# Down-weight sums moved to the tail's second half, and a late scan operand taken from SBUF

## The chip, the cores and the metric

The kernel runs on one core of a Trainium2 chip. The metric is the device time of one execution in microseconds. The engines are named as in the profile: PE (TensorE matmul) and PEld (its weight load), DVE (VectorE), ACT (ScalarE), POOL (GpSimd) and SP, whose queue issues most DMAs.

## The reference

One decoder layer over 2048 tokens of width 1024, all in float32. What the change touches is the stick-breaking attention and the feed-forward part.

```python
z = einsum("bhqd,bhkd->bhqk", qb, kh) * scale          # scale = 1/8, key before query only
log_1m_beta = where(mask, log_sigmoid(-z), 0.0)
between = cumsum(log_1m_beta, reverse) - log_1m_beta
attn = where(mask, exp(log_sigmoid(z) + between), 0.0)  # sigmoid(z) * running product of (1 - sigmoid)
out = einsum("bhqk,bhkd->bhqd", attn, vh)

gt = einsum("bsd,df->bsf", f_in, w_gate)                # d = 1024, f = 2816
up = einsum("bsd,df->bsf", f_in, w_up)
f = einsum("bsf,fd->bsd", silu(gt) * up, w_down)
h = h + rmsnorm(f)
```

Around it stand a norm and an input projection, a gated convolution of width 31 over half of the mixing channels, and an output projection of convolution and attention side by side.

## The kernel before, in words

Matrix products in full precision are made of three: each operand is split into a rounded part H and a remainder L (ACT makes H, DVE or POOL makes L), and PE adds L·H, H·H and H·L in one PSUM bank.

**The trunk.** Tokens come in four groups of 512. The list `PLAN` (line 39) walks through main steps: `prep` and `in` (input projection) for each group, `mixc`/`outc` and `mixa`/`outa` (the convolution's and the attention's half of the output projection), and pieces of the feed-forward (`fprep`, `c11`, `p4`). Each has a cost, and the running sum of costs is a position. Three side generators are drawn along: the attention, the convolution's taps, and `sums`. For each a line of points (`ATTN`, `TAPS`, `SUMS`, lines 69 to 71) says which share of it is to be done at which position; `beside` steps a side until it has reached its share. This sets the order in which instructions are written. A scheduler then reorders them by its own timeline, except where `keep_in_program_order` holds them.

**The attention** (`attn`, line 534) goes group by group, head by head, and for each head through the key chunks from the diagonal to the first; a head and a chunk make a unit of four steps. A step of `scores` multiplies into a bank `z` (two banks), lets ACT take sigmoid(-z) into `om` and sigmoid(z) into `A`, lets DVE run a scan over `om` backwards (line 572), and POOL multiplies `A` by the scanned `om`. The scan is a multiply with the second step bypassed, so its second tensor is read and not used: it is a broadcast of z's first column, from PSUM. Its first element is the previous chunk's product, put there by small POOL copies (`pv`, lines 567 and 575). A step of `values` then transposes `A` on PE (`at`), splits it into TH and TL, and multiplies with V into `o`. After a head come `pf` (fold of halves), and after each pair of heads a norm (`ot`) and a transpose back (`po`, `ma`). The attention of the last group feeds the last half of the output projection, in the tail's first lines.

**The feed-forward** uses a Strassen-like scheme of seven products per 2x2 block. So sums and differences of weight blocks are needed beforehand: `sums` (line 838) makes them on POOL, from pieces of 128x512 that SP loads, and stores them to DRAM: for `w_gate` and `w_up` under the key "S", for `w_down` under "wd". Three buffers `sum` are in use. There are 15 units of work for each of 11 blocks (`HF`), 10 for the first two matrices and 5 for the down matrix, spread along `SUMS`.

**The tail.** When the attention is done, its PSUM pools close. `five` (line 1096) makes five products for each of 44 blocks (token groups 0 and 2, each standing for two groups of 512; 11 column blocks; gate and up). Blocks 0 to 21 are the first half, 22 to 43 the second. A block's weights come by SP into `raw`, ACT makes wH, POOL makes wL (line 1067), and PE and DVE are held in program order. `behind` and `todo` place other work behind a block's second product. Results for the down product are kept in a list `late` and stored by `flush`, two per product. The buffers `x2` (two each of xH and xL) hold operands of products 6 and 5 in the first half and are free in the second.

**The last stage** (from line 1229) makes the seven down products: `fetch` (line 1244) loads a weight piece and a piece of u, and makes their H and L in buffers taken from `x2`; PE accumulates in `dps`.

Of the kernel before, what the change touches and what calls it, by code (L numbers as in the profile page):

```python
# [9 lines left out]
F32 = mybir.dt.float32  # L10
# [55 lines left out]
    ("outc", 3, 22),  # L66
)

ATTN = ((46, 0.0), (890, 1.0))
TAPS = ((30, 0.0), (130, 0.168), (170, 0.25), (260, 0.418), (300, 0.5), (410, 0.668), (450, 0.75), (650, 0.918), (700, 1.0))  # L70
SUMS = ((330, 0.0), (900, 1.0))

# [66 lines left out]
def layer_kernel(ctx: ExitStack, tc: tile.TileContext, x, xT, g_pre_mix, w_in, conv_w, conv_b, ln_g, ln_b,  # L139
# [394 lines left out]
    def attn(g):  # L534
# [20 lines left out]
        def scores(u, j):  # L555
            hd_ = heads[u["h"]]
            diag = u["c"] == g
            w = (j + 1) * P if diag else G
            K = u["K"]
            z = pp.tile([P, G], F32, tag="z", name="z")  # L560
            js = slice(j * P, (j + 1) * P)
            nc.tensor.matmul(z[:, 0:w], hd_["QL"][:, js], K[:, 0:w], start=True, stop=False)  # L562
            nc.tensor.matmul(z[:, 0:w], hd_["QH"][:, js], K[:, 0:w], start=False, stop=True)  # L563
            if diag:
                nc.vector.tensor_tensor(z[:, w - P:w], z[:, w - P:w], msk, ALU.add)  # L565
            om = ap.tile([P, G + 1], F32, tag="om", name="om", bufs=NOM)
            nc.gpsimd.tensor_copy(om[:, G:G + 1], hd_["prev"][j])
            nc.scalar.activation(om[:, G - w:G], z[:, 0:w], AF.Sigmoid, scale=-0.125)  # L568
            a = ap.tile([P, G], F32, tag="A", name="A", bufs=NA)
            nc.scalar.activation(a[:, 0:w], z[:, 0:w], AF.Sigmoid, scale=0.125)  # L570
            r = om[:, G - w:G + 1][:, ::-1]
            nc.vector.tensor_tensor_scan(r, r, z[:, 0:1].to_broadcast([P, w + 1]), one, ALU.mult, ALU.bypass)  # L572
            nc.gpsimd.tensor_tensor(a[:, 0:w], a[:, 0:w], om[:, G - w + 1:G + 1], ALU.mult)  # L573
            pv = sp.tile([P, 1], F32, tag="pv", name="pv", bufs=8)
            nc.gpsimd.tensor_copy(pv, om[:, G - w:G - w + 1])
            hd_["prev"][j] = pv
            u["A"].append(a)
            return w
# [175 lines left out]
    def four(t):  # L754
        return [t[:, i, :] for i in range(4)]
# [80 lines left out]
    def sums():  # L836

        def piece(w, j, e):
            t = fup.tile([P, G], F32, tag="sum", name="sum", bufs=3)
            nc.sync.dma_start(t, w[j][:, e * G:(e + 1) * G])  # L840
            return t

        late = []

        def combine(c, a, b, op, *key):
            nc.gpsimd.tensor_tensor(c, a, b, op)  # L846
            late.append((c, *key))

        def flush(n):
            while len(late) > n:  # L850
                t, kind, *key, m = late.pop(0)
                if kind == "S":
                    ns = (6, 7) if m in (6, 7) else (5, 3)
                    part(t, ns.index(m), 2, kind, *key, ns)
                else:
                    store(t, kind, *key, m)

        for j in range(HF):
            for i, w in enumerate(W):
                a21, a22, a11 = piece(w, j + HF, 0), piece(w, j + HF, 1), piece(w, j, 0)  # L860
                yield 1
                combine(a22, a21, a22, add, "S", i, j, 5)
                yield 1
                combine(a21, a21, a11, sub, "S", i, j, 7)
                combine(a11, a22, a11, sub, "S", i, j, 6)
                yield 1
                flush(0)
                a12 = piece(w, j, 1)
                yield 1
                combine(a12, a12, a11, sub, "S", i, j, 3)  # L870
                yield 1
                flush(0)
        for j in range(HF):
            b12, b11, b22 = piece(w_down, j, 1), piece(w_down, j, 0), piece(w_down, j + HF, 1)
            yield 1
            combine(b11, b12, b11, sub, "wd", j, 5)
            yield 1
            combine(b12, b12, b22, sub, "wd", j, 7)
            combine(b22, b22, b11, sub, "wd", j, 6)
            yield 1  # L880
            flush(0)
            b21 = piece(w_down, j + HF, 0)
            yield 1
            combine(b21, b21, b22, sub, "wd", j, 4)
            yield 1
            flush(0)

    def input_sums(g, k, tmp, banks=bank, t4=None):

# [56 lines left out]

    attn_s = Side(chain(attn(g) for g in range(NG)), 1 / (2 * NH * P * sum(16 * g + 10 for g in range(NG))), ("attn",))
    taps_s = Side(chain(taps(g) for g in range(NG)), 1 / (NG * (CB * CW + 3 * (TAPLAG + LAG * TT))), ("taps", "conv"))
    sums_s = Side(sums(), 1 / (15 * HF))
    fns = {"prep": (prep, 8), "qkv": (lambda g: inproj(g, qkv), 12), "gv": (lambda g: inproj(g, gv), 8),  # L950
           "in": (lambda g: inproj(g, both), 20),
           "mixc": (lambda g: mixed(g, 0), 1), "outc": (lambda g: outproj(g, 0), 4),
# [45 lines left out]
    with ExitStack() as E:  # L998
# [113 lines left out]
        def five(early, todo):  # L1112
# [85 lines left out]
                fn(*args)  # L1198
            next(more_h.pop())
            assert next(more, None) is None  # L1200
            for _ in range(9):
                flush(2)

        operands(0, [(6, x2), (5, x2), (7, e[4:6]), (3, e[0:2])])
        R = []
        last = NG - 2

        def steps():

# [18 lines left out]
        todo = {n: [(next, more)] * (1 if n < 5 else 2 - n % 2) for n in range(17)}  # L1228
        todo[17] = todo[18] = [(next, more)]
        todo[2 * HF - 1] = [(operands, last, [(3, e[0:2])], nc.gpsimd)]  # L1230
        five({2 * HF - 1: [(operands, last, [(7, e[4:6])])]}, todo)


# [164 lines left out]
```

## Time and profile before

| | |
|---|---|
| runs | 2579.35 us median of 3 (2574.46 to 2581.54) |
| the profiled execution's own time | 2579.23 us |
| its span, first to last instruction | 2577.5 us |
| mean granted TensorE clock | 0.977 |
| DVE, ACT, POOL busy | 70%, 50%, 58% |
| DMA in all | 657.32 MB, 255 GB/s |

A matmul of 512 columns has a duration of about 0.40 us in the rows, but they are pipelined and start about 0.23 us apart. Rows of a group give the line, the engine and the operation, the output and inputs by the program's names, the shapes and the count; then the busy time in us, the mean of one in ns, and the idle time of the engine just before, with what ended it. A row of waits names the waiting engine and line, and behind the arrow who ended the wait.

### The profile page before, as it was taken

The page shows a single profiled execution, that of the slowest core. Times are in us where ns is not written, and L with a number is a line of the kernel's source. Part 1 is how long each engine was busy: PE and PEld are TensorE (multiplying, and loading weights), DVE is VectorE, ACT ScalarE, POOL GpSimd, SP SyncE. Part 2 cuts the span into 40 slices and gives each one's busy share as a digit, 9 for nine tenths or more (in the row PEclk, how much of TensorE's full clock was granted, in tenths as well). Part 3 has the DMA queues.
Part 4 walks back from the last instruction along what each step waited for, and adds up shares of the span by engine and source line. Part 5 has one row for each costly group of instructions (what it writes and reads, how often), then busy time and mean ns, then how long its engine had stood idle before and what let it go on. Part 6 is the DMA issues. An engine that isn't in the chain of part 4 may idle for free.

```text
span 2577.5 us, 35682 instructions
## 1 busy us (share of the span) xinstructions
PE 2430.0 (94%) x11156; PEld 1963.3 (76%) x11156; DVE 1793.3 (70%) x2321; ACT 1291.5 (50%) x2398; POOL 1482.5 (58%) x1844
## 2 busy tenths in 40 slices
PE   7999989998999998999999979999999999998997
PEld 6878767776777776887788857777788878887886
DVE  5797689967997798887544547766655655557556
ACT  4455555655555655667666645332332233454543
POOL 5764668556755776639533228755443444567556
PEclk9999989998999899999999989999999999999999
DMA  9989877988898998857777746977656667668655
GB/s 360 303 301 311 287 244 260 369 262 272 273 328 287 314 329 285 275 189 230 263 257 243 242 140 235 340 265 234 213 189 201 199 200 266 195 189 286 204 188 171
DMA packets 289182, 657.32 MB, mean 255 GB/s; under 512 B 33888, under 2 KB 42080, under 8 KB 288992
## 3 DMA queue, kind: packets, MB, share of 16 engines
q1 hardware_dynamic: 264704, 622.01, 72.0%
q10 hardware_dynamic: 24288, 33.04, 3.5%
q8 instruction: 88, 1.44, 0.2%
q14 instruction: 102, 0.84, 0.1%
HBM read 460.92 MB, written 193.99 MB: 254 GB/s over the span
## 4 chain that ended last, share of the span: by engine, by line
PE 52%; DVE 11%; POOL 5%; DMA 4%; issue 3%; ACT 2%; SPq 0%; POOLq 0%; ACTq 0%; DVEq 0%
PE b L762 17%; PE dps L762 13%; PE c L762 8%; DVE cv L476 3%; DVE om L572 2%; PE at L589 2%; PE p L762 1%; PE ops L688 1%; PE ops L689 1%; PE ops L690 1%; PE o L595 1%; PE z L562 1%; PE o L594 1%; PE z L563 1%; DVE TL L249 1%
## 5 line engine op out<-in xcount | busy, mean ns | idle before, releaser
L573 POOL TENSOR_TENSOR A<-A,om 128x512 f32<-128x512 f32 (+2 forms) x320 | 313.7, 980 | 415.9 <-DVE om L572 364.3
L572 DVE TENSOR_TENSOR_SCAN om<-om,one,z 128x513 f32<-128x513 f32 (+2 forms) x320 | 351.3, 1112 | 114.5 <-ACT A L570 103.2
L1067 POOL TENSOR_TENSOR wL<-raw,wH 128x512 fp32r<-128x512 f32 x176 | 255.6, 1478 | 262.9 <-issue 164.6
L476 DVE SCALAR_TENSOR_TENSOR cv<-glu,cw,cv 128x512 f32<-128x512 f32 x464 | 346.6, 747 | 6.7
L1257 DVE TENSOR_TENSOR xL__22001<-t__22003,xH__22000 128x512 fp32r<-128x512 f32 x154 | 199.3, 1302 | 159.5 <-ACT xH__22000 L1256 159.3
L1255 POOL TENSOR_TENSOR xL__21999<-t__22002,xH__21998 128x512 fp32r<-128x512 f32 x154 | 207.8, 1354 | 173.3 <-ACT xH__21998 L1254 172.7
L256 PE MATMUL inps<-xH,wL 128*128 128x512 f32 x640 | 260.8, 408 | 12.9 <-ACT sg L422 11.0
L249 DVE TENSOR_TENSOR TL<-at,TH 128x512 fp32r<-128x512 f32 (+1 forms) x320 | 188.2, 598 | 110.3 <-ACT TH L248 109.8
L260 PE MATMUL inps<-xL,wH 128*128 128x512 f32 x640 | 258.4, 405 | 0.5 <-DVE xL L392 0.5
L258 PE MATMUL inps<-xH,wH 128*128 128x512 f32 x640 | 258.6, 405 | 0.0
L762 PE MATMUL dps<-xH__21998,xL__22001 128*128 128x512 f32 x616 | 240.9, 391 | 8.1 <-DVE xL__22001 L1257 7.2
L568 ACT ACTIVATE om<-z 128x512 f32<-128x512 f32 (+2 forms) x320 | 171.6, 539 | 153.0 <-DVE z L565 70.8
L762 PE MATMUL dps<-xL__21999,xH__22000 128*128 128x512 f32 x616 | 240.6, 391 | 2.2 <-POOL xL__21999 L1255 2.2
L762 PE MATMUL dps<-xH__21998,xH__22000 128*128 128x512 f32 x616 | 240.2, 390 | 0.0
L846 POOL TENSOR_TENSOR sum<-sum 128x512 f32<-128x512 f32 x132 | 171.8, 1302 | 89.3 <-DMA sum<-in_w_up_dram 33.4
L248 ACT ACTIVATE TH<-at 128x512 fp32r<-128x512 f32 (+1 forms) x320 | 168.2, 547 | 106.3 <-PE at L589 102.4
L1254 ACT ACTIVATE xH__21998<-t__22002 128x512 fp32r<-128x512 f32 x154 | 97.1, 631 | 231.9 <-POOL xL__21999 L1255 151.5
L589 PE MATMUL at<-idr,A 128*128 128x128 f32 x1088 | 192.1, 280 | 10.5 <-POOL A L573 9.3
L210 ACT ACTIVATE wH<-raw 128x1024 fp32r<-128x1024 f32 x156 | 165.8, 1065 | 53.5 <-DMA raw<-in_w_in_dram 19.1
L570 ACT ACTIVATE A<-z 128x512 f32<-128x512 f32 (+2 forms) x320 | 168.4, 542 | 21.0 <-PE at L589 13.6
L589 PEld LDWEIGHTS at<-idr,A 128*128 128x128 f32 x1088 | 142.0, 144 | 48.5 <-POOL A L573 12.4
L1066 ACT ACTIVATE wH<-raw 128x512 fp32r<-128x512 f32 x176 | 101.1, 623 | 154.8 <-PE b L762 77.1
(296 smaller groups left out, 6226.3 us busy)
## 6 DMA issues: line engine op xcount, KB each, us to landing
wL<-wL SPq DMA_DIRECT2D x156, 512.0 KB, 5.2
raw<-in_w_in_dram SPq DMA_DIRECT2D x80, 512.0 KB, 6.0
t__22003<-u SPq DMA_DIRECT2D x154, 256.0 KB, 2.8
c<-c ACTq DMA_DIRECT2D x88, 256.0 KB, 4.6
t__22002<-wd SPq DMA_DIRECT2D x88, 256.0 KB, 2.9
K<-kd SPq DMA_DIRECT2D x80, 256.0 KB, 4.6
V<-vd SPq DMA_DIRECT2D x80, 256.0 KB, 4.5
u<-accf SPq DMA_DIRECT2D x22, 768.0 KB, 4.2
```

The costliest lines, as they stand in the source:

```text
L249: nc.vector.tensor_tensor(L, ps, H.bitcast(F32), ALU.subtract)
L256: nc.tensor.matmul(ps, WL[:, kc], aH[t](k), start=k == 0, stop=False)
L258: nc.tensor.matmul(ps, WH[:, kc], aH[t](k), start=False, stop=False)
L260: nc.tensor.matmul(ps, WH[:, kc], aL[t](k), start=False, stop=k == KT - 1)
L476: nc.vector.scalar_tensor_tensor(to, gl[c][:, k:k + G], cw[:, c, k:k + 1], a, ALU.mult, ALU.add))
L572: nc.vector.tensor_tensor_scan(r, r, z[:, 0:1].to_broadcast([P, w + 1]), one, ALU.mult, ALU.bypass)
L573: nc.gpsimd.tensor_tensor(a[:, 0:w], a[:, 0:w], om[:, G - w + 1:G + 1], ALU.mult)
L589: nc.tensor.transpose(pt[:, j * P:(j + 1) * P], u["A"][j][:, b * P:(b + 1) * P], id32)
L762: return nc.tensor.matmul(ps, a, b, skip_group_check=True, **flags)
L1067: nc.gpsimd.tensor_tensor(l, t, f32(h), sub)
L1255: nc.gpsimd.tensor_tensor(WL, w, f32(WH), sub)
L1257: nc.vector.tensor_tensor(UL, t, f32(UH), sub)
```

## The change

Four edits:

1. `ATTN` ends at position 870 instead of 890.
2. The down matrix's part leaves `sums`, whose scale becomes 1/(10·HF); `SUMS` is unchanged.
3. A new generator `down_sums` makes the same sums inside the tail, two steps in each of blocks 22 to 43 and one behind the last: per column block four loads, four POOL operations, four stores through `late`. Its 16 buffers are the slices of `x2`. Its POOL operations are held in program order. Twelve rounds of `flush` instead of nine close the stage.
4. In the last group, for heads 4 to 7, the scan's unused second tensor is a broadcast of `one`, a column of ones in SBUF, instead of z's first column.

```diff
-ATTN = ((46, 0.0), (890, 1.0))
+ATTN = ((46, 0.0), (870, 1.0))
...
+            late = g == NG - 1 and u["h"] >= NH // 2
...
-            nc.vector.tensor_tensor_scan(r, r, z[:, 0:1].to_broadcast([P, w + 1]), one, ALU.mult, ALU.bypass)
+            nc.vector.tensor_tensor_scan(r, r, (one if late else z[:, 0:1]).to_broadcast([P, w + 1]), one, ALU.mult, ALU.bypass)
...
-        for j in range(HF):
-            b12, b11, b22 = piece(w_down, j, 1), piece(w_down, j, 0), piece(w_down, j + HF, 1)
-            yield 1
-            combine(b11, b12, b11, sub, "wd", j, 5)
-            yield 1
-            combine(b12, b12, b22, sub, "wd", j, 7)
-            combine(b22, b22, b11, sub, "wd", j, 6)
-            yield 1
-            flush(0)
-            b21 = piece(w_down, j + HF, 0)
-            yield 1
-            combine(b21, b21, b22, sub, "wd", j, 4)
-            yield 1
-            flush(0)
...
-    sums_s = Side(sums(), 1 / (15 * HF))
+    sums_s = Side(sums(), 1 / (10 * HF))
...
-            for _ in range(9):
+            next(more_wd)
+            for _ in range(12):
                 flush(2)
...
+        def down_sums():
+
+            wd = cycle([p for _ in range(2) for t in operand(*x2, dt=F32) for p in four(t)])
+
+            def piece(j, e, c):
+                t = next(wd)
+                nc.sync.dma_start(t, w_down[j][:, c * G:(c + 1) * G])
+                return t
+
+            def pinned(*args):
+                tc.keep_in_program_order(nc.gpsimd.tensor_tensor(*args))
+
+            def get(j):
+                return piece(j, 0, 1), piece(j, 0, 0), piece(j + HF, 0, 1), piece(j + HF, 0, 0)
+
+            nxt = get(0)
+            yield
+            for j in range(HF):
+                b12, b11, b22, b21 = nxt
+                pinned(b11, b12, b11, sub)
+                late.append([1, b11, "wd", j, 5])
+                yield
+                pinned(b12, b12, b22, sub)
+                late.append([1, b12, "wd", j, 7])
+                yield
+                pinned(b22, b22, b11, sub)
+                late.append([1, b22, "wd", j, 6])
+                yield
+                pinned(b21, b21, b22, sub)
+                late.append([1, b21, "wd", j, 4])
+                yield
+                if j + 1 < HF:
+                    nxt = get(j + 1)
...
+        more_wd = down_sums()
+        for n in range(2 * HF, 4 * HF):
+            todo[n] = todo.get(n, []) + [(next, more_wd)] * 2
```

The scheduler orders the whole trunk anew, so nearly every queue differs. Three places carry the prediction's steps; behind each row stand the engines and DMA queues that it waits for.

PE, end of the attention, before: `ops` is the first half of the last output projection, `z` the last unit's scores, `o`, `at` its values. The last `ops` row and what follows:

```order
L690 MATMUL ops_17368<-wL_17245,xH_17206 128x512
L562 MATMUL z_16877<-K_16873,QL_16280 128x512 [waits DMAHW4_49,DVE_49]
L563 MATMUL z_16877<-K_16873,QH_16279 128x512
L594 MATMUL o_16487<-TH_16844,V_16472 128x512 [waits Activation_49]
L562 MATMUL z_16945<-K_16873,QL_16280 128x512 [waits DVE_49]
L563 MATMUL z_16945<-K_16873,QH_16279 128x512
L595 MATMUL o_16487<-TL_16845,V_16472 128x512 [waits DVE_49]
```

PE, the same unit's first scores in the change, in the midst of `ops`:

```order
L691 MATMUL ops_17120<-wL_17027,xH_16988 128x512
L563 MATMUL z_16631<-K_16627,QL_15958 128x512 [waits DMAHW2_49,Activation_49]
L564 MATMUL z_16631<-K_16627,QH_15957 128x512
L563 MATMUL z_16691<-K_16627,QL_15958 128x512 [waits Activation_49]
L564 MATMUL z_16691<-K_16627,QH_15957 128x512
L595 MATMUL o_16209<-TH_16606,V_16194 128x512 [waits Activation_49]
L590 MATMUL at_16643<-idr_72,A_16527 128x128 [waits Pool_49]
L689 MATMUL ops_17134<-wH_17020,xL_16989 128x512 [waits Activation_49]
```

Before, all four z's of the last unit stand behind the last `ops` row and wait for DVE; 60 rows come between that row and the last half of the projection. In the change they wait for ACT and stand ahead of the last `ops` row, behind which 43 rows are left.

POOL in the tail's second half, before, one burst of wL for a block and the start of the next:

```order
L1067 TENSOR_TENSOR wL_21701<-raw2_21633,wH_21700 128x512 [waits DMAHW2_49,Activation_49,Pool_49]
L1067 TENSOR_TENSOR wL_21701<-raw2_21633,wH_21700 128x512 [waits Activation_49]
L1067 TENSOR_TENSOR wL_21763<-raw_21740,wH_21762 128x512 [waits DMAHW5_49,Activation_49,Pool_49]
L1067 TENSOR_TENSOR wL_21763<-raw_21740,wH_21762 128x512 [waits Activation_49]
L1067 TENSOR_TENSOR wL_21797<-raw2_21742,wH_21796 128x512 [waits DMAHW2_49,Activation_49]
```

and in the change:

```order
L1054 TENSOR_TENSOR wL_21732<-raw2_21667,wH_21731 128x512 [waits DMAHW3_49,Activation_49]
L1054 TENSOR_TENSOR wL_21732<-raw2_21667,wH_21731 128x512 [waits Activation_49]
L1206 TENSOR_TENSOR xL__19709<-xL__19709 128x512 [waits Pool_49] x2
L1054 TENSOR_TENSOR wL_21799<-raw_21768,wH_21798 128x512 [waits DMAHW4_49,Activation_49]
L1054 TENSOR_TENSOR wL_21799<-raw_21768,wH_21798 128x512 [waits Activation_49]
```

Two sums now stand between two bursts.

ACT at the start of the last stage, in the change: L1279 makes the H of the weights, L1281 (line 1256 before) the H of u.

```order
L1279 ACTIVATE xH__21958<-t0__21962 128x512 [waits DMAHW7_49]
L1279 ACTIVATE xH__21958<-t0__21962 128x512 [waits DMAHW2_49]
L1281 ACTIVATE xH__21960<-t1__21963 128x512 [waits DMAHW5_49,DMAHW3_49,DMAHW6_49,DMAHW1_49,Pool_49]
L1281 ACTIVATE xH__21960<-t1__21963 128x512
L1281 ACTIVATE xH__21960<-t1__21963 128x512 [waits DMAHW0_49]
```

The first H of u waits for POOL and for the stores of the last column block's four sums, which lie in its buffer; before, it waited for its own load alone.

## The prediction

> **What bounds the kernel now.** I read the page's first lines, then TensorE's busy time by stage, then who ended TensorE's idle time in the stages that the change touches, and last the built order of before and of the change.
>
> ```profile
> span 2577.5 us, 35682 instructions
> PE 2430.0 (94%) x11156; PEld 1963.3 (76%) x11156; DVE 1793.3 (70%) x2321; ACT 1291.5 (50%) x2398; POOL 1482.5 (58%) x1844
> ```
>
> TensorE (PE) is the bound: 147.5 us of the span are not covered by it, and that is all that an edit which adds and removes no matmul can win, beside time at a lower granted clock. The stages (columns: PE, weight loads, DVE, ACT, POOL busy, then granted clock, DMA share, GB/s):
>
> ```profile
> 658.00:1044.00 386.00, 355.82 (x1735) 286.16 (x1734) 341.86 (x470) 220.45 (x411) 262.94 (x381) 0.98 0.88 303
> 1044.00:1248.00 204.00, 200.59 (x988) 163.73 (x987) 154.66 (x201) 139.50 (x264) 132.21 (x209) 1.00 0.67 221
> 1248.00:1485.00 237.00, 231.87 (x1144) 189.51 (x1143) 118.53 (x154) 155.23 (x284) 82.64 (x184) 1.00 0.76 258
> 1485.00:1531.00 46.00, 32.01 (x126) 24.01 (x125) 23.92 (x32) 23.64 (x42) 9.26 (x16) 0.74 0.39 132
> 1600.00:1823.00 223.00, 215.41 (x917) 171.30 (x917) 158.24 (x187) 73.68 (x131) 136.60 (x93) 0.99 0.81 282
> 1823.00:2131.00 308.00, 302.71 (x1298) 244.08 (x1298) 180.56 (x220) 91.36 (x160) 132.32 (x92) 1.00 0.61 199
> 2131.00:2577.50 446.50, 425.39 (x1860) 349.13 (x1859) 263.84 (x234) 201.77 (x380) 266.08 (x210) 0.99 0.65 214
> ```
>
> 658 to 1044 is where the sums of the down weights run now (the last 44 of L846's 132); PE lacks 30.2 us there. 1248 to 1485 holds nearly all of the scans that the change calls late, beside plain matmuls; PE lacks 5.1 us. 1485 to 1531 is the handover from the attention to the tail: 14.0 us idle, and the granted clock falls to 0.74. 1823 to 2131 is the tail's second half, which receives the moved work; PE lacks 5.3 us there.
>
> **Part one: the late scans give the z bank back.** PE's waits, first of 658 to 1044 (its first, sixth and eighth rows), then of 1248 to 1485, then of the handover (waited for: us in total, times, longest):
>
> ```profile
> PE z L562 <- DVE om L572: 13.9, 16, 1.6
> ...
> PE at L589 <- POOL A L573: 1.1, 1, 1.1
> ...
> PE c L762 <- POOL wL L214: 0.8, 1, 0.8
> ```
>
> ```profile
> PE z L562 <- DVE om L572: 4.6, 6, 2.0
> ```
>
> ```profile
> PE po L627 <- DVE ot L619: 5.0, 1, 5.0
> PE z L562 <- DVE om L572: 3.8, 1, 3.8
> PE ops L688 <- DVE e__17289 L527: 2.0, 1, 2.0
> PE o L595 <- DVE TL L249: 1.7, 1, 1.7
> ```
>
> There are two z banks. Before, a bank is free only when the scan has read its unused operand from it; in the change the last reader is the second sigmoid on ACT (L570), and the order shows the z matmul waiting for ACT instead of DVE. In 1248 to 1485 the wait of 4.6 us is the stage's loss but for half a microsecond, and ACT (155 of 237 us busy) runs a sigmoid ahead of the scan. The gain is between 0 (ACT is as late as the scan) and 4.6; I take 4, since the scan (1.27 us, below) follows the sigmoid that now releases the bank.
>
> At the handover the order says more than the wait. In both orders the last attention matmul comes after the last matmul of the first half of the output projection (`ops`, from xH and xL), so the last rows run with nothing beside them: 60 rows before, 43 after.
>
> ```profile
> 1494.27 0.39 PE L562 MATMUL z<-K,QL 128*128 128x512 f32 x1
> ...
> 1500.26 0.80 PE L562 MATMUL z<-K,QL 128*128 128x512 f32 x1 [3.80 <-DVE om L572]
> ...
> 1501.29 0.63 PE L594 MATMUL o<-TH,V 128*128 128x512 f32 x1
> ```
>
> Before, that bare stretch begins at 1494.27 with the z's of the last unit; eight value steps remain from 1501.29. After, all four z's stand among `ops` matmuls and the stretch begins inside the first of the eight. So 7.0 us of it go. The 17 rows that move among the covered matmuls still cost PE its time: some 8 z and 3 o rows of 512 columns at about 0.23 us from start to start, and six short ones, about 3 us. Net 4. Bounds: 0 if the scans' results are the limit in either order, 14.0 if all idle time of the stage went; the wait of 5.0 for `ot` and the chain behind it are untouched, so I stay at 4.
>
> What the new operand costs on DVE the trace of before does not show, since no scan there reads a second tensor from SBUF. The nearest rows: the scan, its multiply on POOL, and TL in 1248 to 1510; then from the tail's second half (1830 to 2115) an addition with an operand from PSUM, and one with both from SBUF:
>
> ```profile
> L572 DVE TENSOR_TENSOR_SCAN om<-om,one,z 128x513 f32<-128x513 f32 x52 | 64.8, 1270 | 49.4 <-ACT A L570 48.5 <-POOL msa L191 0.4 <-POOL om L567 0.3
> L249 DVE TENSOR_TENSOR TL<-at,TH 128x512 fp32r<-128x512 f32 x52 | 34.6, 678 | 49.4 <-ACT TH L248 49.4
> ...
> L573 POOL TENSOR_TENSOR A<-A,om 128x512 f32<-128x512 f32 x52 | 56.8, 1093 | 125.6 <-DVE om L572 114.1 <-PE c L762 4.6 <-PE o L594 3.2
> ```
>
> ```profile
> L1074 DVE TENSOR_TENSOR b<-b,glu 128x512 f32<-128x512 f32 x26 | 18.2, 699 | 33.7 <-PE b L762 33.7
> ...
> L1074 DVE TENSOR_TENSOR accf<-accf 128x512 f32<-128x512 f32 x7 | 12.1, 1726 | 0.1
> ```
>
> The same addition takes 0.70 us with one operand in PSUM and 1.73 us with both in SBUF, beside POOL's bursts: about 1.03 us are waiting, and POOL's own work can stretch too. So a late scan costs between nothing (POOL idle: it is busy 83 of 237 us) and 1.09 us, the length of one multiply of A. A unit of four steps then needs at most 4 x (1.27 + 1.09 + 0.68) = 12.2 us if scan, multiply and TL never overlap. There are 64 late scans, 16 units, in 262 us: 16.4 us a unit. The collisions fit beneath the `c` matmuls, and I take 0; the other end is a rival.
>
> The Trainium skill, "SBUF — State Buffer", section "Who interferes with whom", says that a VectorE instruction with two SBUF inputs and a GpSimd instruction that reads SBUF block each other for a whole instruction. By that rule this edit is a loss wherever scans are the limit; the 0.70 and 1.73 us rows agree with it, and none of before shows it on a scan.
>
> **Part two: what leaves the middle.** The sums, and POOL's waits in 658 to 1044:
>
> ```profile
> L846 POOL TENSOR_TENSOR sum<-sum 128x512 f32<-128x512 f32 x132 | 171.8, 1302 | 89.3 <-DMA sum<-in_w_up_dram 33.4 <-DMA sum<-in_w_gate_dram 27.6 <-issue 11.8
> ```
>
> ```profile
> POOL A L573 <- DVE om L572: 78.2, 36, 5.8
> POOL sum L846 <- DMA sum<-in_w_down_dram: 8.1, 5, 4.3
> ```
>
> 44 x 1.302 = 57.3 us leave POOL, 22% of its 262.9, with 8.1 us in which POOL stood for their loads; 44 loads and 44 stores of 256 KB leave SP and the DMA queue. The sums of w_gate and w_up keep their places in the built order relative to the attention. The 30.2 us of idle are mostly not POOL's: z waits for scans, 13.9, while POOL is named for 1.9. But a scan's first element is copied by POOL (L567, L575), behind whatever POOL does. Bounds: a gain of 13.9 if all these waits go; a loss of 8.2 if DVE, 341.9 of 386 us busy, is the limit, because ATTN's new end asks for 844/824 = 2.4% more attention per position. I take POOL's 22% of 13.9, a gain of 3.
>
> **Part three: what arrives in the tail.** POOL in 1830 to 2115, and SP's longest wait in 1823 to 2131:
>
> ```profile
> L1067 POOL TENSOR_TENSOR wL<-raw,wH 128x512 fp32r<-128x512 f32 x84 | 120.3, 1459 | 163.0 <-issue 156.9 <-ACT wH L1066 6.0
> ```
>
> ```profile
> SPq L1055 <- POOL wL L1067: 92.9, 19, 6.1
> ```
>
> POOL sits idle about 8 us before each burst of four wL, and the order puts two sums behind each burst (2 x 1.30, at most 2 x 1.75). So they hide in that gap; without it each block would lose 2.6 us, 22 x 2.6 = 57. Behind a waiting sum stand the next wL, and PE waits for those; but the loads of the sums are issued about three groups ahead, sixteen pieces deep. On SP 88 DMAs join the loads of `raw`, `a` and `glu`, which already stand up to 6.1 us behind wL. The first half shows the price of a fuller queue: DMA share 0.81 against 0.61, and 7.6 us idle in 223, against 5.3 in 308. At that rate the second half would lack 10.5, so the bounds are 0 and +5.2. I take +2, as 22.5 MB over 308 us would lift 199 to about 270 GB/s and the first half had other waits as well.
>
> At the last stage the new buffers' release is on the way: its first activations of u (L1256) now wait for the last `wd` store.
>
> ```profile
> 2106.89 6.41 POOL L1067 TENSOR_TENSOR wL<-raw,wH 128x512 fp32r<-128x512 f32 x4 [8.65 <-issue]
> 2119.51 1.30 POOL L1255 TENSOR_TENSOR xL__21999<-t__22002,xH__21998 128x512 fp32r<-128x512 f32 x1 [6.21 <-ACT xH__21998 L1254]
> ```
>
> ```profile
> t__22002<-wd SPq DMA_DIRECT2D x88, 256.0 KB, 2.9
> ```
>
> ```profile
> 2133.62 0.40 PE L762 MATMUL dps<-xH__21998,xL__22001 128*128 128x512 f32 x1
> ```
>
> POOL is done with wL at 2113.3, five sums and one xL take until about 2122, the store (like a load, 2.9 us) lands near 2126, and activation and subtraction need some 2 us: ready by 2129 for a matmul at 2133.6. Cover 4 us, cost 0.
>
> **The sum.** -4 (z waits) -4 (handover) -3 (middle) +2 (tail) = -9. The profiled span of 2577.5 becomes 2568.5; that execution took 2579.23, 1.7 more than its span, and the median is 2579.35. Forecast 2570.
>
> **The rivals.** *Nothing in sum.* The order still lets the attention end behind the projection, so the ATTN edit may change nothing, and the tail may pay 5 for what the z waits return (4): about 2577. For it: the handover's chain from `oT` to `po` (5.0) is untouched. Against it: the z waits are named by the trace and have a new releaser.
>
> *Slower: late scans and POOL exclude each other.* It decides where a unit takes over 16.4 us, or no matmul is left to cover: the last four units, 16 scans x 1.09 = 17.4 us, with the z gains lost; with -3 and +2 that is about +16: 2596. For it: the 1.73 us row. Against it: POOL's 35% load there, and 12.2 us against 16.4. The Trainium skill's rule cited above is this rival's ground.
>
> *The middle opens up.* All 13.9 of z waits there go with POOL's load, and with them the clock's 0.98: -14 -4 -4 +2 = -20, 2559. Against it: POOL is named for 1.9 us only.
>
> *The change doesn't do what it says:* ACT becomes the late releaser, and the z waits stay under its name; then -4 -3 +2, 2574, within the first rival's reach.
>
> **How the numbers follow.** Forecast 0.48 (own range 2561 to 2578), nothing in sum, with the last rival, 0.28, slower 0.14, the middle 0.10. 0.3% is 7.7 us, about what a measurement of this kernel can tell from no change: 2571.6 and 2587.1. Of the forecast's 0.48 some 0.39 lies below 2571.6, with the middle 0.10 and little else: faster 0.50; slower 0.13; same 0.37. The range reaches from the middle's case, with a few microseconds more, to the near edge of the slower one: 2554 to 2586, which leaves out under 0.2.
>
> **What would show it.** Right: no z wait on DVE behind 1248, a handover near 40 us, POOL below 58% in the middle with shorter z waits, no PE wait on POOL in the second half, and dps without a gap before it. Scans above 1.3 us at the handover, or a TL or A that lags, show the slower rival; waits of b on DVE glu or POOL wL in the second half show a dearer tail. The forecast is wrong if the middle's idle time grows under the new pacing, which reorders every queue from the start.

## Result: 2559 us, and the profile after

| | before | after |
|---|---|---|
| median (range), runs | 2580.24 us (2574.46 to 2584.46), 6 | 2559.27 us (2551.76 to 2560.57), 6 |
| ratio after/before, 95% interval | | 0.9907 [0.9894, 0.9921] |
| profiled execution's own time | 2579.23 us | 2551.76 us |

The change is faster by 21 us by the medians and by 24 by the ratio, more than twice the forecast of 9. The profiled execution of after is the shortest of its six, 7.5 us below their median, so the 27.6 us between the two spans are more than the change is worth. The head of after's page:

```profile
span 2549.9 us, 35685 instructions
PE 2422.0 (95%) x11156; PEld 1956.1 (77%) x11156; DVE 1806.7 (71%) x2321; ACT 1291.8 (51%) x2398; POOL 1518.6 (60%) x1844
```

PE is idle for 2549.9 - 2422.0 = 127.9 us, against 147.5 before: 19.6 less. The other 8.0 us are busy time: the same 11156 matmuls ran at a mean granted clock of 0.983 instead of 0.977. POOL is busy for 36 us more, though no operation of it was added: the same ones run longer. A moved sum takes about 1.5 us in the tail against 1.30 before, the multiply of `A` 1.17 against 1.12 over the whole run.

The stages of after by time, in the columns of the prediction's stage rows. First the prediction's middle, then its late scans, the handover, the tail's second half with the end of its first, and the last stage:

```profile
658.00:1044.00 386.00, 368.24 (x1812) 297.77 (x1811) 331.84 (x468) 227.50 (x419) 213.73 (x336) 0.99 0.77 260
1244.00:1455.00 211.00, 208.58 (x1038) 170.51 (x1038) 123.85 (x154) 143.94 (x266) 99.74 (x177) 1.00 0.77 254
1455.00:1502.00 47.00, 35.45 (x156) 27.05 (x155) 23.00 (x31) 26.79 (x47) 11.32 (x18) 0.87 0.51 176
1797.00:2103.00 306.00, 306.00 (x1315) 247.31 (x1315) 193.16 (x221) 91.34 (x160) 195.18 (x136) 1.00 0.77 267
2103.00:2549.90 446.90, 423.56 (x1850) 347.29 (x1848) 263.74 (x236) 201.78 (x380) 268.07 (x210) 0.99 0.66 216
```

PE's idle time goes from 30.2 to 17.8 us in the middle, from 5.1 to 2.4 with the late scans, from 14.0 to 11.6 in the handover, from 5.3 to nothing in the second half, where POOL went from 132 to 195 us; the last stage has 23.3 instead of 21.1. PE's waits in after, 658 to 1044:

```profile
PE z L563 <- DVE om L573: 5.6, 8, 1.3
PE o L596 <- DVE TL L249: 4.5, 5, 1.7
```

The z waits there were 13.9. In 1244 to 1455 no z wait is left, of 4.6; this is the longest wait of all there:

```profile
PE c L763 <- DVE xL L269: 1.2, 1, 1.2
```

At the handover the chain behind `ot` stays as it was:

```profile
PE po L628 <- DVE ot L620: 5.0, 1, 5.0
PE o L595 <- ACT TH L248: 2.7, 2, 2.2
PE ops L689 <- DVE e__17069 L527: 2.0, 1, 2.0
```

What the new operand costs, which nothing of before could show: the full scans of the whole run, with z and with `one`, and then, of 1240 to 1480, POOL's multiply behind them:

```profile
L573 DVE TENSOR_TENSOR_SCAN om<-om,one,z 128x513 f32<-128x513 f32 x172 | 216.9, 1272 | 52.7 <-ACT A L571 39.6 <-POOL om L568 6.3 <-POOL wL L227 3.5
L573 DVE TENSOR_TENSOR_SCAN om<-om,one 128x513 f32<-128x513 f32 x52 | 69.0, 1349 | 36.4 <-ACT om L569 35.6 <-POOL pv L576 0.5
```

```profile
L574 POOL TENSOR_TENSOR A<-A,om 128x512 f32<-128x512 f32 x53 | 68.7, 1301 | 75.7 <-ACT A L571 34.4 <-DVE om L573 10.6 <-ACT om L569 9.4
```

A scan grew by 0.08 us on the mean, a multiply from 1.09 to 1.30; 52 x 0.08 = 4 us on DVE and 53 x 0.21 = 11 us on POOL, both under the `c` matmuls.

### The profile page after: what moved, and what is told of

Its sections match the earlier page's. It is cut to its first block, busy times and chain, and to the rows that moved or that the text cites. A ratio compares the mean times of both kernels' runs of the same rounds, so it can differ in the third digit from the quotient of the medians.

```text
span 2549.9 us, 35685 instructions
## 1 busy us (share of the span) xinstructions
PE 2422.0 (95%) x11156; PEld 1956.1 (77%) x11156; DVE 1806.7 (71%) x2321; ACT 1291.8 (51%) x2398; POOL 1518.6 (60%) x1844
## 5 line engine op out<-in xcount | busy, mean ns | idle before, releaser
L574 POOL TENSOR_TENSOR A<-A,om 128x512 f32<-128x512 f32 (+2 forms) x320 | 327.4, 1024 | 357.5 <-DVE om L573 234.9
L573 DVE TENSOR_TENSOR_SCAN om<-om,one,z 128x513 f32<-128x513 f32 (+3 forms) x256 | 278.0, 1098 | 62.4 <-ACT A L571 48.6
L1279 ACT ACTIVATE xH__21958<-t__21962 128x512 fp32r<-128x512 f32 x154 | 97.1, 631 | 229.0 <-POOL xL__21959 L1280 142.3
L571 ACT ACTIVATE A<-z 128x512 f32<-128x512 f32 (+2 forms) x320 | 168.1, 540 | 10.8 <-PE at L590 10.5
L847 POOL TENSOR_TENSOR sum<-sum 128x512 f32<-128x512 f32 x88 | 115.6, 1313 | 74.6 <-DMA sum<-in_w_up_dram 42.4
```

The lines of the kernel that those rows point to most:

```text
L573: nc.vector.tensor_tensor_scan(r, r, (one if late else z[:, 0:1]).to_broadcast([P, w + 1]), one, ALU.mult, ALU.bypass)
```

## The experiments

Three edits of the change can stand alone: the sums' new place (**sums**), ATTN's end at 870 (**pace**), the operand from SBUF (**late**). All combinations were run. In each, the sums' edit is the change's second and third item as a whole. The others are these lines, given as they stand without the edit and with it:

```diff
-ATTN = ((46, 0.0), (890, 1.0))
+ATTN = ((46, 0.0), (870, 1.0))
```

```diff
-z[:, 0:1].to_broadcast([P, w + 1])
+(one if late else z[:, 0:1]).to_broadcast([P, w + 1])
```

To compare them, each trace is cut at the same matmuls: the first of the third output projection (A), the first of the last output projection (B), the first of the tail's `five` (C), and the end. "Left" is the number of scans that start after B, that is, how much attention still runs when nothing but half a projection is there to cover it. "Idle to A" is PE's idle time from the end of the last input projection to A. Ratios are against runs of before on the same chip, with 95% intervals; the stage times are of one profiled execution each, which lay up to 10 us from its median.

| kernel | ratio [interval] | idle to A | B at | left | B to last half | C at | C to end |
|---|---|---|---|---|---|---|---|
| before | 1 | 16.5 | 1462.6 | 12 | 64.1 | 1551.0 | 1026.5 |
| late | 0.9988 [0.9974, 1.0001] | 16.3 | 1464.4 | 4 | 43.4 | 1532.0 | 1032.3 |
| pace | 1.0048 [1.0031, 1.0065] | 14.2 | 1459.7 | 16 | 70.0 | 1554.4 | 1032.5 |
| pace, late | 1.0034 [1.0017, 1.0051] | 15.5 | 1473.3 | 9 | 54.2 | 1553.0 | 1032.8 |
| sums | 1.0000 [0.9985, 1.0014] | 5.7 | 1426.0 | 24 | 93.8 | 1545.1 | 1026.7 |
| sums, late | 0.9958 [0.9944, 0.9973] | 5.9 | 1433.6 | 20 | 81.8 | 1541.0 | 1030.0 |
| sums, pace | 0.9949 [0.9930, 0.9967] | 8.5 | 1442.6 | 16 | 71.3 | 1539.2 | 1025.8 |
| after (all) | 0.9907 [0.9894, 0.9921] | 8.0 | 1442.5 | 9 | 55.3 | 1523.2 | 1026.7 |

("B to last half" ends where the last projection's last half begins, which needs the whole attention; 24 to 26 us of matmuls lie between it and C in every kernel.)

**One edit alone.**

> Only the down sums moved to the tail (ATTN ends at 890, scans as before). Load theory (the middle gains because POOL and the queue lose 57 us of sums and 88 transfers): 13 to 18 us faster than before, about 2565, with TensorE's idle time from 658 to 1044 us about halved from 30 us. The forecast's own steps (middle -3, tail +2): about 1 us faster, 2579. Order theory (the gain in the middle comes from the new pacing, which reorders the queues): within 5 us of before.

Measured 2579.14 us (12 runs): no difference, as the order theory and the forecast's own steps had it. Yet PE's idle time from 658 to 1044 us is halved, 30.2 to 14.6, as the load theory had it: the trace shows a gain and its loss. Before, from the end of the input projection to A, and then from B to the last half:

```profile
871.10:1103.60 232.50, 215.99 (x1056) 173.25 (x1054) 206.58 (x283) 142.09 (x264) 154.29 (x219) 0.97 0.88 304
1462.60:1526.60 64.00, 50.05 (x220) 38.92 (x218) 31.94 (x41) 36.68 (x67) 17.38 (x34) 0.84 0.47 163
```

The same two stages with only the sums moved:

```profile
865.90:1065.60 199.70, 194.04 (x956) 155.75 (x955) 163.13 (x233) 122.44 (x226) 117.62 (x164) 1.00 0.88 306
1426.00:1519.80 93.80, 73.25 (x321) 52.38 (x318) 55.66 (x72) 55.79 (x105) 34.64 (x71) 0.90 0.40 138
```

PE's idle time to A falls by 10.8 us and the clock rises from 0.97 to 1.00. But the built order also shifts a hundred matmuls, nearly all the attention's, out of this stage (44 scans start in it instead of 56), and as much attention comes after B, where little covers it: B comes 36.6 us earlier, and some 30 of these go into a longer handover, with 20.5 us idle.

> Only ATTN's end from 890 to 870. Load theory: within 4 us of before, 2576 to 2584, the idle time of the middle still near 30 us. The forecast's own steps: no change, 2580. Order theory: 8 to 18 us faster.

Measured 2590.7 us (6 runs): the pace alone is a loss of 0.48%, which none of the three theories had. Its price stands in the stage of the third input projection, before and with the pace alone:

```profile
434.40:696.10 261.70, 242.40 (x1144) 194.01 (x1142) 223.62 (x319) 147.82 (x278) 166.03 (x259) 0.96 0.87 294
```

```profile
426.40:704.80 278.40, 253.51 (x1184) 201.94 (x1184) 232.29 (x335) 153.96 (x292) 175.02 (x272) 0.96 0.86 289
```

Forty matmuls more, 16.7 us longer, idle from 19.3 to 24.9. And it buys nothing later: 16 scans are left at B instead of 12.

> Only the late scans' operand from SBUF. The forecast's own steps (z waits -4, handover -4): 8 us faster, 2572, with no z wait on the scan behind 1248 us, and the stages before it as before. Load theory: the same 5 to 8 us. Rival (scan and POOL exclude each other and cost what the bank gains): 0 to +5.

Measured 2576.48 us (12 runs), 0.12% faster, with an interval that still holds no change; the 8 us of the forecast's own steps did not come. The handover is the shortest of the four with the sums in the trunk:

```profile
1464.40:1507.80 43.40, 32.84 (x157) 26.10 (x155) 18.19 (x25) 24.52 (x42) 8.92 (x10) 0.88 0.65 229
```

Its profiled execution is 10 us below its median, so the 19 us by which its C is earlier than before's must not be read as its worth.

**Two edits together.**

> Sums moved and late scans, ATTN ends at 890: the change without its pacing. Load theory: the whole gain of the change but for 2 us, about 2560. The forecast's own steps: 9 us faster, 2571. Order theory: at most 10 us faster, since the pacing is missing.

Measured 2568.87 us (6 runs), 0.42% faster: near the forecast's own steps and the order theory's limit, and not the load theory's 2560.

> The change without the late scans: sums moved, ATTN ends at 870, every scan reads z. Handover theory (the moved sums save about 10 us of idle in the middle, but leave more of the attention for the handover, and the pacing brings it forward again): 6 to 16 us faster than before, 2564 to 2574, with fewer scans behind the start of the last output projection than the 24 of the moved sums alone. Additive theory (moved sums 0, pacing +11, as measured alone): 2590. Late-scan theory (nothing pays without them): 2580 or more.

Measured 2566.69 us (7 runs), 0.51% faster with 16 scans left: as the handover theory had it, against the other two. From B to the last half, against 93.80 us with 20.5 idle when the pace is left at 890:

```profile
1442.60:1513.90 71.30, 57.34 (x253) 42.94 (x251) 39.30 (x54) 41.60 (x79) 22.62 (x46) 0.87 0.45 163
```

> ATTN ends at 870 and late scans, with the sums left in the trunk: the change without the moved sums. Handover theory: the middle keeps its 14 to 16 us of idle, so 2575 to 2590, no faster than before by more than 5. Additive theory (pacing +11, late -3): 2588. If the sums were not needed for the gain: 2560 to 2570.

Measured 2587.68 us (9 runs): within what the handover theory and the additive theory gave, so it does not part them; that the sums were not needed is ruled out.

What follows from the eight. If the edits were terms of a sum, the three alone would give 1 - 0.0012 + 0.0048 + 0.0000 = 1.0036, slower by 9 us. The whole change is faster by 24. The gap is two interactions, each of which the table gives twice:

- sums with pace: 0.9949 - 1.0048 - 1.0000 + 1 = -0.0099 without late, 0.9907 - 1.0034 - 0.9958 + 0.9988 = -0.0097 with it; some 25 us;
- sums with late: 0.9958 - 1.0000 - 0.9988 + 1 = -0.0030, and -0.0028 with the pace; some 7 us;
- pace with late: -0.0002 and 0.

Each of these is a sum of four ratios whose intervals reach some 0.0015 to either side, so it is uncertain by about 0.003. The first is clear of that; the second is as large as its uncertainty, and only its coming out twice speaks for it.

The column "left" says why the first is so. With the sums in the trunk, the earlier pace raises it (12 to 16, and 4 to 9 with late). With the sums gone it falls (24 to 16, and 20 to 9). At 870 it is the same with and without the sums. So moving the sums brings B forward in any case, by 17 to 37 us, and all four kernels of it have 5.7 to 8.5 us idle to A against 14.2 to 16.5; but at 890 it throws the attention back by 12 to 16 scans, and the pace at 870 takes that back. Why the scheduler's order lets the attention lag at 890 was not tried.

**What left the trunk, taken apart.** The down sums are arithmetic on POOL and transfers. Each half was left in the trunk by itself.

```diff
-            b12, b11, b22 = piece(w_down, j, 1), piece(w_down, j, 0), piece(w_down, j + HF, 1)
+            t = [fup.tile([P, G], F32, tag="sum", name="sum", bufs=3) for _ in range(3)]
...
-            combine(b11, b12, b11, sub, "wd", j, 5)
+            nc.gpsimd.tensor_tensor(t[0], lng, lnb, sub)
...
-                nc.sync.dma_start(w, stored["wd", j, n])
+                nc.sync.dma_start(w, w_down[j][:, 0:G])
```

> As before, but the down sums' 44 POOL operations in the trunk work on constants in SBUF and their 88 transfers are left out; the last stage reads plain pieces of w_down, as many bytes, so the result is not the layer's. If POOL's 57 us cause the idle of the middle: 14 to 16 us of idle between the end of the input projections and the third output projection stay. If the transfers do: 5 to 8, as with the sums moved.

Measured 2602.87 us (4 runs), 1.0096 [1.0073, 1.0119]; idle to A 10.0 us, C at 1563.5. But the stage to A is no test of the load here: all 44 operations ran between 651 and 787 us, before it begins at 876. Where they do stand, from the first matmul of the second output projection to the end of the last input projection, PE is idle for 21.7 us, against 15.1 with only the sums moved. The kernel with only the sums moved, then this one:

```profile
615.10:865.90 250.80, 235.71 (x1130) 190.24 (x1131) 219.01 (x311) 142.49 (x263) 129.93 (x222) 0.97 0.67 224
618.40:876.10 257.70, 236.03 (x1098) 189.63 (x1097) 222.72 (x301) 135.94 (x253) 176.91 (x252) 0.94 0.64 212
```

```diff
-            combine(b11, b12, b11, sub, "wd", j, 5)
+            late.append((b11, "wd", j, 5))
...
```

> As before, but the down sums' 44 POOL operations are left out while their 44 loads and 44 stores stay, so the result is not the layer's. If POOL's 57 us cause the idle of the middle: 5 to 8 us of idle in that stage instead of 16. If the transfers or their place in SP's queue do: 14 to 16 stay.

Measured 2588.8 us (7 runs), 1.0049 [1.0027, 1.0070]. The 6.1 us idle to A say nothing about the transfers either: all but two of the 88 were issued between 651 and 870 us, before that stage. The stage in which they do stand:

```profile
617.50:870.60 253.10, 238.01 (x1130) 192.21 (x1130) 219.65 (x311) 142.35 (x264) 129.48 (x221) 0.97 0.89 307
```

With only the sums moved the DMA share is 0.67 there, and PE's idle time is the same 15.1 us: where they stand, the transfers made no idle time that this trace shows. A third kernel has no down sums anywhere; it is the one with only the sums moved, less the moved work:

```diff
-        more_wd = down_sums()
-        for n in range(2 * HF, 4 * HF):
-            todo[n] = todo.get(n, []) + [(next, more_wd)] * 2
...
-                nc.sync.dma_start(w, stored["wd", j, n])
+                nc.sync.dma_start(w, w_down[j][:, 0:G])
```

> Leaves out part of the computation: the 44 sums of the down weights are computed nowhere, neither in the trunk nor in the tail; the last stage reads plain pieces of w_down in their place. ATTN ends at 890 and the scans read z, so its trunk is that of the kernel with only the sums moved; the two differ by the moved work alone. Theory one (the tail's second half carries the 44 sums, 44 loads and 44 stores for nothing, since TensorE is busy there without a gap): the same time as with only the sums moved, 2579 within 4 us, ratio to before 0.998 to 1.001. Rival (the prediction's term, +2 with bounds 0 and +5.2): 2 to 5 us faster than that kernel, ratio 0.998 or less.

Measured 2585.69 us (12 runs), 1.0032 [1.0020, 1.0044]: neither theory. Without the moved work the kernel is slower than with it by 0.32%, 8 us. Up to the tail the two traces agree: 24 scans left, 93.7 us from B to the last half, C at 1546.9 (with the moved work 1545.1). In the tail they part; the same 314 us of both, first with the moved work, then without:

```profile
1820.00:2134.00 314.00, 314.00 (x1351) 254.24 (x1350) 200.21 (x230) 94.45 (x166) 199.92 (x138) 1.00 0.76 268
```

```profile
1820.00:2134.00 314.00, 308.69 (x1317) 248.98 (x1316) 182.00 (x224) 91.26 (x160) 132.46 (x92) 0.99 0.59 200
```

PE's waits of the second:

```profile
PE b L762 <- POOL wL L1053: 3.0, 1, 3.0
PE b L762 <- DVE glu L1060: 2.3, 1, 2.3
```

These two, 5.3 us, are the whole difference in this stretch, and before has both, though its tail is no longer than with the moved work (1026.5 and 1026.7 us): other waits are shorter in its order. The queues behind them, before: POOL at the halfway of the tail, and DVE at its end, with the matmul that waits at each place.

```profile
1823.72 6.37 POOL L810 TENSOR_TENSOR e__19805<-sumin,e__19804 128x512 fp32r<-128x512 f32 x4 [4.77 <-ACT e__19804 L809]
1830.05 5.45 POOL L1067 TENSOR_TENSOR wL<-raw,wH 128x512 fp32r<-128x512 f32 x4
```

```profile
1831.82 0.50 PE L762 MATMUL b<-t__19403,wL 128*128 128x512 f32 x1 [3.02 <-POOL wL L1067]
```

```profile
2124.43 2.85 DVE L1257 TENSOR_TENSOR xL__22001<-t__22003,xH__22000 128x512 fp32r<-128x512 f32 x2
2127.20 1.48 DVE L1074 TENSOR_TENSOR glu<-b,glu 128x512 f32<-128x512 f32 x2
```

```profile
2127.94 0.73 PE L762 MATMUL b<-e__18328,a22h 128*128 128x512 f32 x2 [2.28 <-DVE glu L1074]
```

And with only the sums moved, the same places:

```profile
1821.05 1.30 POOL L810 TENSOR_TENSOR e__19585<-sumin,e__19584 128x512 fp32r<-128x512 f32 x1 [4.77 <-ACT e__19584 L809]
1822.30 3.44 POOL L1053 TENSOR_TENSOR wL<-raw,wH 128x512 fp32r<-128x512 f32 x2
1825.70 4.69 POOL L810 TENSOR_TENSOR e__19585<-sumin,e__19584 128x512 fp32r<-128x512 f32 x3
```

```profile
2116.94 0.69 DVE L1060 TENSOR_TENSOR glu<-b,glu 128x512 f32<-128x512 f32 x1 [2.09 <-PE b L762]
2119.74 0.69 DVE L1060 TENSOR_TENSOR glu<-b,glu 128x512 f32<-128x512 f32 x1 [2.11 <-PE b L762]
2123.85 1.89 DVE L1281 TENSOR_TENSOR xL__21961<-t__21963,xH__21960 128x512 fp32r<-128x512 f32 x3 [1.62 <-ACT xH__21960 L1280]
```

Before, POOL did four operand subtractions in a row and then the wL for which PE stood; with the sums in its queue the built order puts two wL among them. And the last stage's first xL, whose buffers the moved sums now hold until their last store, stand behind the `glu` for which PE waits, not ahead of it.

Against this kernel the two halves can be priced, at ATTN's 890 and with the order that each got: the arithmetic on POOL 1.0096 - 1.0032 = 0.64%, 16 us, clear of both intervals; the transfers 1.0049 - 1.0032 = 0.17%, 4 us, which is not clear, since the intervals overlap. They don't add up to before, which has both and is faster than either; left at B are 24 scans in all three, but 12 in before.

The arithmetic does cost PE idle time where it stands: 21.7 us against 15.1, or 11.2 with no moved work, two kernels of the same trunk whose difference shows what one trace can tell. What made 14 to 16 us idle to A is not settled. Before has 13 of its 44 sums in that stage, and neither half kernel has any there. The stage also holds less attention: 56 scans start in it before and 48 with the pace, but 44 to 46 in the four kernels with the sums moved. That is a rival which no run here parts from POOL's load. Nor is it shown that POOL's small copies ahead of the scans carry the wait. What DVE's scans wait for in before's 658 to 1044 is ACT by name, and POOL in no row:

```profile
DVE om L572 <- ACT A L570: 6.7, 6, 2.5
```

**The operand's price where POOL is busy.**

```diff
-            late = g == NG - 1 and u["h"] >= NH // 2
+            late = True
```

> The changed kernel with every scan, not only the late ones, reading its unused operand from SBUF. Theory one (a scan with SBUF operands and GpSimd's work hold each other up, which costs nothing only where GpSimd is lightly loaded): the trunk's 162 other full scans grow from 1.27 us towards 1.5 to 2 us where GpSimd is 55% busy, z and o waits grow, 5 to 20 us slower than the changed kernel, 2564 to 2580. Rival (what counts is that the z bank comes free earlier): the waits of z for scans that are left before 1244 us go, up to 15 us faster than the changed kernel, 2545 to 2558.

Measured 2581.97 us (10 runs), 1.0020 [1.0005, 1.0035]: 0.0113 or 29 us slower than the change, more than theory one's 5 to 20. The full scans up to 1240 us, those which in the change read z at 1.27 us; then PE's longest, third and seventh-longest waits of the whole run; then from B to the last half:

```profile
L573 DVE TENSOR_TENSOR_SCAN om<-om,one 128x513 f32<-128x513 f32 x172 | 279.0, 1632 | 14.9 <-ACT om L569 14.2
```

```profile
PE o L596 <- DVE TL L249: 30.8, 30, 4.1
...
PE z L563 <- ACT A L571: 8.3, 11, 1.6
...
PE o L595 <- ACT TH L248: 6.0, 7, 1.7
```

```profile
1508.00:1531.70 23.70, 23.70 (x108) 19.16 (x106) 7.07 (x11) 14.07 (x24) 1.83 (x2) 1.00 0.85 325
```

172 x (1.632 - 1.272) = 62 us go to DVE, and TL, behind the scans in DVE's queue, becomes what PE waits for: 30.8 us instead of 11.9. The rival is half right too: the z waits on scans, 23.3 us in after, are gone, 8.3 on ACT come in their place, and no scan at all is left at B. But what that frees is less than what the longer scans cost: B comes 65 us later than in after. The run decides for contention. Single scans confirm it: with `one`, those during which POOL ran nothing took 1.27 to 1.29 us (23 of the 52 full ones in the change, 35 of the 172 here), and every one above 1.30 (8 there, 84 here) overlapped work on POOL. The Trainium skill, "SBUF — State Buffer", section "Who interferes with whom", has a VectorE instruction with two SBUF inputs contend with a GpSimd instruction that reads SBUF; these scans agree, 1.63 us against 1.27, and 1.35 where POOL has less to do.

**The pace itself**, with everything else as in the change:

```diff
-ATTN = ((46, 0.0), (870, 1.0))
+ATTN = ((46, 0.0), (880, 1.0))
```

> The changed kernel with ATTN ending at 880, between the 890 of before and the 870 of the change. Theory one (with the sums gone from the trunk the attention lags the projections, and the pace pays by the number of scans left behind the start of the last projection): 20 scans are left at 890 and 9 at 870, so some 14 here, and the time lies between 2569 and 2559, near 2564. Rival (the pace acts only by chance of the built order, which it reshuffles): the time falls outside 2556 to 2572, with no relation to the scans left.

Measured 2570.03 us (12 runs), 0.9973 [0.9959, 0.9987]. Not 14 scans are left, as I had put it between the two ends, but 20, as at 890; B to the last half takes 81.4 us, and the time is near that of 890 (0.9958). Left does not move evenly with ATTN's end, and the time went with left.

> The changed kernel with ATTN ending at 850. Theory one (scans left at the handover are what the pace pays for): fewer than 9 scans are left, the handover is shorter than 55 us, and what is gained there is partly lost in the third input projection, which grew by 7 us from 890 to 870: 2552 to 2562. Rival (denser attention fills GpSimd and VectorE in the input projections, and that is dearer than the handover): the third input projection grows by more than 10 us again and the time is 2564 or more.

Measured 2563.0 us (6 runs), 0.9946 [0.9926, 0.9965]. 4 scans are left and B to the last half takes 46.4 us, 8.9 less than in after; but the third input projection, 270.0 us in after, is now this:

```profile
432.50:717.50 285.00, 259.71 (x1207) 204.24 (x1207) 236.41 (x338) 161.28 (x307) 166.26 (x279) 0.96 0.76 259
```

15 us are lost there, and B comes 22.7 us later. Both theories have a half: the handover does get shorter, and the denser trunk takes more than that. 870 is the best of the four ends that were run, and no kernel here beats the change.

## Why the prediction was right, and where it was not

The time, 2559, lies in the range 2554 to 2586 and the sign is the likeliest one; it lies below the forecast's own range of 2561 to 2578. The sum of -9 was less than half of what came, and it was the width given to the range for the case "the middle opens up" that held the time. Some terms came out right for other reasons, which is luck:

- **z waits, -4.** Right in the mechanism. The waits of 4.6 us are gone, no wait on ACT's sigmoid took their place, and PE's idle time with the late scans fell by 2.7. As an edit alone the late scans were worth 3 us, not clear of noise.
- **Handover, -4.** The gain came, and part of the last units now stands among covered matmuls, as argued: PE's idle time went from 14.0 to 11.6, though the stage as cut by time is 47 us long and not near 40. But it was credited to the operand alone, so the size is partly luck. With the sums moved and the pace left, the handover would have been 81.8 us with it and 93.8 without; the pace is what keeps it at 55.3.
- **Middle, "I take POOL's 22% of 13.9, a gain of 3".** This is the term that was mis-sized. PE's idle time there fell by 12.4 and the z waits by 8.3 of 13.9. It came with the sums: with them alone moved 14.6 us are idle from 658 to 1044, with the pace alone 28.6. The step that failed is the one from a share of POOL's busy time to the same share of the waits. How much of the fall is POOL's lighter load and how much the attention that the new order moved out of the stage is open. The case called "the middle opens up" had the size (2559) and part of the ground: z waits down by 60%, not by all, and the clock from 0.98 to 0.99.
- **ATTN's end.** I priced it only as a possible loss in the middle, up to 8.2, and let the rest stand. It is a loss alone (0.48%, twice in the table) and a gain of 0.51% once the sums are gone. A sum of terms, each worked out with the others left as before, can't hold that; the order of the change as a whole, which stood in the built program, could.
- **Tail, +2.** Wrong sign in the second half. The gap ahead of each burst of wL did hide the sums, as argued, and PE has no idle time there at all. What I left out is that a moved operation changes its queue's order: it parted four subtractions that held wL up, and its buffers delayed the xL that held `glu` up. 5.3 us came back. In after's first half other waits grew by 3.2, so the tail as a whole is as long as in before's profile (1026.7 and 1026.5); against the other kernels without the sums there, 1032 to 1039, it is shorter.
- **Last stage, 0.** The first `dps` starts without a gap. The stage took 446.7 us against 443.9; kernels with the sums in the tail have 446.7 to 448.5, the others 443.1 to 446.4, so 1 to 3 us may be its price.
- **"Late scans and POOL exclude each other".** The mechanism is real and the bound of 1.09 us a scan was far off: 0.08 on DVE, 0.21 on POOL, under cover. The sign named for it, late scans above 1.3 us, did show (1.35 on the mean), and still cost PE nothing that its waits show. Taken to all scans it costs 29 us.
- **"ACT becomes the releaser".** Not in the change; with every scan on `one`, ACT is named for 8.3 us.

By pairs: without late, sums and pace were priced at -3 + 2 = -1 and measured -0.51%, -13 us; late on top was priced at -8 and measured 0.9949 to 0.9907, -11.

## What to carry to other kernels

Where a scheduler writes the order, a table of pacing and the work that it paces are one edit: run them together, and run the combinations before crediting either. Count what is left of the side work when the last cover begins; here the handover's length followed that count, from 23.7 us at none to 93.8 at 24 scans. And work put into an engine's idle gaps is never only its own duration: ask which operations it now stands between, and which later ones its buffers hold back.

## What the hardware showed beyond that

- The contention of a scan with both operands in SBUF depends on the neighbour's load, not on the form alone: 1.27 us with an operand in PSUM, the same 1.27 to 1.29 with both in SBUF while POOL ran nothing, 1.35 on the mean beside a POOL that was busy 46% of the time, 1.63 beside one busy 69%, single ones up to 3.5; POOL's multiply behind the late scans went from 1.09 to 1.30.
- 44 loads and 44 stores of 256 KB raised the DMA share from 0.67 to 0.89 in the stage where they stood, and PE's idle time there stayed at 15.1 us; their price in the whole kernel's time, 0.17%, is not clear of noise.
- The executions of one kernel lie up to 18 us apart (2568.89 to 2587.15 for before, in 18 runs on one chip). Single traces put the change at 27.6 us and late alone at 13; the medians say 21 and 3. Stage lengths of one trace settle where time goes, and not how much of it.
